# Sums of the up-projection's weights made ahead of time on GpSimd and kept in DRAM, and gate weights in three smaller buffers

## The chip, the cores and the metric

One core of one Trainium2 chip runs the whole program. Its engines work side by side: TensorE (PE, with PEld for its weight loads), VectorE (DVE), ScalarE (ACT), GpSimd (POOL) and SyncE (SP), which here issues every DMA. Each engine takes its instructions strictly in order, and an instruction that waits for a semaphore holds everything behind it on its engine; SP's list of DMAs is such a queue too. The metric is the device time of one execution in microseconds. Lower is better.

## The reference

One layer of a bidirectional encoder on two sequences of 512 tokens, width 1024, in float32:

```python
h = rmsnorm(x, g_attn) * (1 + sc1) + sh1
z = h @ w_in                                  # mixers A and B, and two gates of 1024 columns each
oa = window_attention(rope(qa), rope(ka), va) # mixer A: 8 heads, 2 key heads, band of +-128
ob = dense_attention(qb, kb, vb)              # mixer B: 8 heads, low-rank q and kv, full 512 x 512
mix = sigmoid(gla) * (oa @ w_o_a) + sigmoid(glb) * (ob @ w_o_b)
x = x + gt1 * (mix @ w_out)
h2 = rmsnorm(x, g_ffn) * (1 + sc2) + sh2
u = dwconv(h2 @ w_up, conv_w, conv_b)         # w_up: 1024 x 5632, convolution of width 3 over tokens
ua, ug = split(u)                             # 2816 columns each
x = x + gt2 * ((silu(ug) * ua) @ w_down)
```

## The kernel before

**Products.** Every large product is made of three TensorE products of float32r operands: each operand is split into a rounded high part and the rest, and high x high, high x low and low x high are added up in PSUM. A split is a cast or copy for the high part (ACT, or POOL at line 69) and a subtraction for the rest (DVE, or POOL at line 72 or 922).

**Stages, in order.** Input projection of mixers A and B (0 to about 216 us of the span); attention of both mixers, with the gates' projection woven in (to about 584 us); branch outputs, gated sum and output projection (to about 767 us); up-projection with convolution and gating (to about 1211 us); down-projection.

**Attention.** The work goes by units: one unit is one head and 128 queries, 64 units of mixer B (`PairB`) and then 64 of mixer A (`GroupA`). A unit's scores go to PSUM; DVE takes the maximum (L501), ACT the exponential (L504), DVE the reciprocal of the sum (L505), and POOL multiplies the row by it (L506, tile `p`). TensorE transposes `p` (L512) `LAG = 3` units after the scores. Between them `fill(5)` puts five matmuls of the gate projection (`psg`, L491) into every unit. The gate weights come in halves of 128 columns, `wg_raw`, 512 KB each; POOL splits each by two L69 and two L72 instructions. Before, two buffers hold a pair of halves each.

**Up-projection.** The two sequences and the two halves of the weights are multiplied with seven products in place of eight, for each of 22 blocks `c` of 128 columns. Four of the seven weight operands are sums of the four quarters a1, a2 (of the value half) and g1, g2 (of the gate half): `sf[0] = g1 + g2`, `sf[1] = sf[0] - a1`, `sf[2] = a1 - g1`, `sf[3] = a2 - sf[1]`. `weights_rest` (L931 to L943) makes them on POOL, 128 x 512 each, then `split_w` (L919) casts on ACT (L921) and subtracts on DVE or POOL (L922). The results `px`, `py`, `pz` are copied out of PSUM by ACT (`copied`, L960), convolved (L966 to L969), gated and stored to `g_d`. Raw weights pass through six buffers `wraw`, split ones through eight, `wt`. The first two products of blocks 0 to 3 are made early (`EARLY`), so right after that four blocks of five products each follow one another.

**What sets the order.** The text above is written in one order, but a scheduler lays out each engine's list in advance: by its own estimates of durations it takes, whenever an engine is idle, the next instruction whose inputs are there. So an instruction that is ready early moves far ahead of its place in the text. The lists are fixed on the chip. A buffer that is used in turn makes its next writer wait for its last reader: the load of a tile waits for the store of the tile two before it, where there are two buffers.

Of the kernel before, what the change touches and what calls it, by code (L numbers as in the profile page):

```python
# [8 lines left out]
F32 = mybir.dt.float32  # L9
F32R = mybir.dt.float32r  # L10
# [7 lines left out]
NB = 2  # L18
S = 512
TOK = NB * S  # L20
NT = S // 128
KD = D // 128
# [11 lines left out]
NP = FF // 128  # L34
# [5 lines left out]
def encoder_block(ctx, tc, x, c_t, w_ada0, b_col, w_ada, b_ada, cols, w_z, w_g, gains, tabs, sink,  # L40
# [11 lines left out]
    g_d = dram.tile([NB, NP, 128, S], F32, name="g_d")  # L52
    x1_d = dram.tile([TOK, D], F32, name="x1_d")
    gt_d = dram.tile([2, NB, D], F32, name="gt_d")

    ident = const.tile([128, 128], F32, name="ident")
    make_identity(nc, ident)
# [10 lines left out]
    def split_pool(hi, lo, raw, in_order=False):  # L68
        ins = G.tensor_scalar(out=hi, in0=raw, scalar1=1.0, scalar2=0.0, op0=ALU.mult, op1=ALU.add)  # L69
        if in_order:  # L70
            tc.keep_in_program_order(ins)
        G.tensor_sub(lo, raw, hi.bitcast(F32))  # L72
# [389 lines left out]
    with ExitStack() as st:  # L462
# [6 lines left out]

        def gates():  # L470

            def load(f):
                w = gw.tile([128, 2, 2, KD, 128], F32R, name=f"wg{f % 2}")
                for m in range(2):
                    raw = gw.tile([128, KD, 128], F32, name="wg_raw", bufs=2)
                    SY.dma_start(raw, w_g[f, :, m])
                    for k in range(0, KD, 4):
                        split_pool(w[:, 0, m, k:k + 4], w[:, 1, m, k:k + 4], raw[:, k:k + 4])
                return w

            w_next = load(0)
            for f in range(KD):
                w = w_next
                for q in range(4):
                    m, b = divmod(q, 2)
                    if q == 1 and f + 1 < KD:
                        w_next = load(f + 1)
                    ps = psg.tile([128, S], F32, name="psg")
                    for k in range(KD):
                        for n, (wl, hl) in enumerate(((0, h_hi), (0, h_lo), (1, h_hi))):  # L490
                            PE.matmul(ps, lhsT=w[:, wl, m, k, :], rhs=hl[b][:, k, :],  # L491
                                      start=k == 0 and n == 0, stop=k == KD - 1 and n == 2)
                            yield
                    go = gw.tile([128, S], F32, name="go", bufs=2)
                    A.copy(go, ps)
                    SY.dma_start(gate_d[b, f, :, m], go)

        def softmax(ps, n, plen):

# [179 lines left out]

        blocks = [PairB(b, g) for b in range(NB) for g in range(BH // 2)] + [GroupA(b, g) for b in range(NB) for g in range(AKV)]  # L680
        gate = gates()

        def fill(n):
            for _ in range(n):
# [8 lines left out]
        for n in range(len(todo) + LAG + 2):  # L693
            if n < len(todo):
                blk, u, first = todo[n]
                if first:
                    for _ in nxt:
                        pass
                    bi, since = blocks.index(blk), 0
                    nxt = blocks[bi + 1].prep() if bi + 1 < len(blocks) else iter(())  # L700
                scored.append((blk, u, blk.scores(u)))
            fill(5)
            for blk_, h in heads:
                blk_.values(h)
            heads = []
            if scored and (n >= LAG):
                blk_, u_, p_ = scored.pop(0)
                h = blk_.spread(u_, p_)
                if h is not None:
                    heads.append((blk_, h))  # L710
            if n < len(todo):
                if since >= blk.prep_from:
                    next(nxt, None)
                since += 1
        for _ in gate:
            pass


# [4 lines left out]
        return pm.tile([128, 512], F32, name=name, tag="bank")  # L723

    def wraw(src):
        r = wp.tile([128, 512], F32, name="wraw", bufs=6)
        SY.dma_start(r, src)
        return r

# [86 lines left out]
    with ExitStack() as s0:  # L816
        wk = s0.enter_context(tc.tile_pool(name="wkx", bufs=1))

        def tmp(tag):
            return wk.tile([128, S], F32, name=f"tmp_{tag}", bufs={"cc": 6, "sf": 5}.get(tag, 2))  # L820

        x1 = [mblk("x1_0", "st", [128, NT, D], F32), mblk("x1_1", "pt", [128, NT, D], F32)]
        ss = wk.tile([128, 2 * NT, 2], F32, name="ss2")
# [98 lines left out]
            lo_eng.tensor_sub(w[:, 1], raw, w[:, 0].bitcast(F32))  # L922
            return w.rearrange("p a (k n) -> p a k n", k=4)

        def weights_first(c):
            for q in range(2):
                yield split_w(wraw(w_up[c, 0, q]), G)

        def weights_rest(c, raws=None):  # L931
            a1, a2 = raws or (wraw(w_up[c, 0, 0]), wraw(w_up[c, 0, 1]))
            g1, g2 = wraw(w_up[c, 1, 0]), wraw(w_up[c, 1, 1])
            sf = [tmp("sf") for _ in range(4)]
            G.tensor_add(sf[0], g1, g2)
            G.tensor_sub(sf[1], sf[0], a1)
            yield split_w(sf[1], V)
            yield split_w(sf[0], V)
            G.tensor_sub(sf[2], a1, g1)
            yield split_w(sf[2], V)  # L940
            G.tensor_sub(sf[3], a2, sf[1])
            yield split_w(sf[3], V)
            yield split_w(g2, G)  # L943

        def weights_all(c):
            raws = (wraw(w_up[c, 0, 0]), wraw(w_up[c, 0, 1]))
            for r in raws:
                yield split_w(r, G)
            yield from weights_rest(c, raws)

        def product(ps, w, name, add=False, sl=slice(0, S)):
            for i in range(4):
# [191 lines left out]
```

## Time and profile before

| what | value |
|---|---|
| time, median of 3 runs (lowest to highest) | 1456.73 us (1453.19 to 1458.41) |
| time of the profiled execution | 1456.77 us |
| its span, first to last instruction | 1455.0 us |
| busy, share of the span | PE 96%, PEld 79%, DVE 69%, ACT 47%, POOL 41% |
| mean granted TensorE clock | 0.992 of full speed |
| read from and written to device memory | 148.39 MB and 44.06 MB |

TensorE is busy nearly everywhere, so the interest lies in the few stretches where it is not, and in what the other engines still have free beside it. A row that gives a line (L922) gives a line of the kernel before; a releaser, as in "<-POOL tmp_sf L936", is what ended an idle time. Matmul durations in the rows overlap: 128 x 512 matmuls follow one another faster than the duration of one says.

### The profile page before, as it was taken

The numbers are of one execution on the slowest core, as the hardware profiler recorded it, in microseconds if no ns is written. First come the engines' busy times: TensorE is split into PE (matmuls) and PEld (weight loads), VectorE is DVE, ScalarE is ACT, GpSimd is POOL, SyncE is SP. The second block draws the span as 40 slices with busy tenths as digits, with TensorE's granted clock in tenths as the row PEclk, the third lists the DMA queues.
The fourth block names the chain that finished last, engine by engine and source line by source line (L and its number), as shares of the span: only waits on it lengthen the run. The fifth ranks groups of instructions, "written<-read, shape, count | busy, mean of one in ns | idle before, by whom it ended". The sixth has DMA issues, their size and how long they took to land.

```text
span 1455.0 us, 20795 instructions
## 1 busy us (share of the span) xinstructions
PE 1391.8 (96%) x7184; PEld 1153.1 (79%) x7184; DVE 1000.3 (69%) x1907; ACT 679.3 (47%) x1385; POOL 596.0 (41%) x592
## 2 busy tenths in 40 slices
PE   5888998999999999999998899999999999999998
PEld 4777776888888888878887767888888888888887
DVE  5788776666678886545479888777777787447433
ACT  3475223666666665422347455555555554212210
POOL 3174023442433442381005755555555545544430
PEclk9999999999999999999999999999999999999999
DMA  8565763322222213655312322222222327646522
GB/s 342 176 216 170 236 239 135 116 88 87 88 87 73 102 64 120 236 176 200 133 39 73 120 74 87 87 82 85 87 85 82 102 73 250 205 148 223 180 87 73
DMA packets 107801, 193.82 MB, mean 133 GB/s; under 512 B 18856, under 2 KB 39592, under 8 KB 104624
## 3 DMA queue, kind: packets, MB, share of 16 engines
q1 hardware_dynamic: 107696, 192.49, 39.8%
q8 instruction: 57, 0.93, 0.3%
q14 instruction: 48, 0.39, 0.1%
HBM read 148.39 MB, written 44.06 MB: 132 GB/s over the span
## 4 chain that ended last, share of the span: by engine, by line
PE 77%; DVE 13%; POOL 3%; ACT 2%; DMA 2%; issue 2%; SPq 0%; ACTq 0%; POOLq 0%; DVEq 0%
PE px L955 13%; PE psg L491 11%; PE py L955 7%; PE psd L79 5%; PE psd L80 5%; PE psd L81 5%; PE pz L955 3%; PE ppt L512 3%; PE ppo L575 2%; PE psx L81 2%; PE psx L80 2%; PE psx L79 2%; PE psz L79 2%; PE psy L81 1%; PE psy L79 1%
## 5 line engine op out<-in xcount | busy, mean ns | idle before, releaser
L955 PE MATMUL px<-t,wt 128*128 128x512 f32 x792 | 191.2, 391 | 7.0 <-ACT tmp_cc L960 6.3
L922 POOL TENSOR_TENSOR wt<-wraw,wt 128x512 fp32r<-128x512 f32 x66 | 92.8, 1410 | 232.2 <-ACT wt L921 232.0
L955 PEld LDWEIGHTS px<-t,wt 128*128 128x128 f32 x792 | 148.0, 188 | 41.1 <-ACT tmp_cc L960 9.5
L491 PE MATMUL psg<-h_hi,wg 128*128 128x512 f32 x512 | 170.2, 397 | 0.0
L506 POOL TENSOR_SCALAR p<-p,l 128x512 f32<-128x512 f32 (+2 forms) x128 | 78.8, 617 | 200.3 <-DVE l L505 125.7
L76 DVE TENSOR_TENSOR wd<-wraw,wd 128x512 fp32r<-128x512 f32 x88 | 93.1, 1098 | 96.4 <-ACT wd L75 96.4
L79 PE MATMUL psd<-wd 128*128 128x512 f32 x352 | 136.9, 389 | 0.0
L80 PE MATMUL psd<-wd 128*128 128x512 f32 x352 | 136.9, 389 | 0.0
L81 PE MATMUL psd<-wd 128*128 128x512 f32 x352 | 136.9, 389 | 0.0
L75 ACT CAST wd<-wraw 128x512 fp32r<-128x512 f32 x88 | 51.3, 620 | 156.1 <-issue 86.9
L491 PEld LDWEIGHTS psg<-h_hi,wg 128*128 128x128 f32 x512 | 95.9, 189 | 18.4 <-POOL wg L69 0.8
L491 PE MATMUL psg<-h_lo,wg 128*128 128x512 f32 x256 | 101.8, 397 | 0.0
L504 ACT ACTIVATE p<-pps,nm 128x512 f32<-128x512 f32 (+2 forms) x128 | 78.2, 611 | 39.3 <-DVE nm L501 31.7
L922 DVE TENSOR_TENSOR wt<-tmp_sf,wt 128x512 fp32r<-128x512 f32 x88 | 82.2, 944 | 12.2 <-ACT wt L921 12.0
L967 DVE SCALAR_TENSOR_TENSOR tmp_u<-tmp_cc,cw,tmp_u 128x511 f32<-128x511 f32 x66 | 64.3, 974 | 37.3 <-ACT tmp_u L966 37.2
L69 POOL TENSOR_SCALAR wd<-wraw 128x512 fp32r<-128x512 f32 x44 | 34.2, 777 | 112.0 <-PE psd L81 63.9
L81 PEld LDWEIGHTS psd<-wd 128*128 128x128 f32 x352 | 66.1, 188 | 13.8
L79 PEld LDWEIGHTS psd<-wd 128*128 128x128 f32 x352 | 66.1, 188 | 13.7
L80 PEld LDWEIGHTS psd<-wd 128*128 128x128 f32 x352 | 66.1, 188 | 13.6
L501 DVE TENSOR_REDUCE nm<-pps 128x1 f32<-128x512 f32 (+2 forms) x128 | 74.7, 584 | 3.1 <-PE pps L81 1.5
L966 ACT ACTIVATE tmp_u<-tmp_cc,cw 128x512 f32<-128x512 f32 x66 | 53.6, 813 | 45.7 <-DMA g_d<-tmp_u 25.6
L72 POOL TENSOR_TENSOR wd<-wraw,wd 128x512 fp32r<-128x512 f32 x44 | 72.7, 1653 | 3.7
(257 smaller groups left out, 3517.8 us busy)
## 6 DMA issues: line engine op xcount, KB each, us to landing
w_ada<-in_w_ada_dram SPq DMA_DIRECT2D x24, 1024.0 KB, 7.1
wraw<-in_w_up_dram SPq DMA_DIRECT2D x96, 256.0 KB, 2.7
wraw<-in_w_down_dram SPq DMA_DIRECT2D x88, 256.0 KB, 3.6
g_d<-tmp_u SPq DMA_DIRECT2D x44, 256.0 KB, 2.4
wraw<-g_d SPq DMA_DIRECT2D x44, 256.0 KB, 2.7
wg_raw<-in_w_g_dram SPq DMA_DIRECT2D x16, 512.0 KB, 3.7
gate_d<-go SPq DMA_DIRECT2D x32, 256.0 KB, 2.0
ldb<-qb_d SPq DMA_DIRECT2D x8, 1024.0 KB, 4.9
```

The costliest lines, as they stand in the source:

```text
L72: G.tensor_sub(lo, raw, hi.bitcast(F32))
L76: V.tensor_sub(lo, raw, hi.bitcast(F32))
L79: PE.matmul(ps, lhsT=lh, rhs=rh, start=first, stop=False)
L80: PE.matmul(ps, lhsT=lh, rhs=rl, start=False, stop=False)
L81: PE.matmul(ps, lhsT=ll, rhs=rh, start=False, stop=last)
L491: PE.matmul(ps, lhsT=w[:, wl, m, k, :], rhs=hl[b][:, k, :], start=k == 0 and n == 0, stop=k == KD - 1 and n == 2)
L501: V.tensor_reduce(nm, ps[:, :n], op=ALU.max, axis=AX.X, negate=True)
L504: A.activation(p[:, :n], ps[:, :n], AF.Exp, bias=nm, accum_out=l)
L506: G.tensor_scalar(out=p[:, :plen], in0=p[:, :plen], scalar1=l, scalar2=1.0, op0=ALU.mult, op1=ALU.mult)
L922: lo_eng.tensor_sub(w[:, 1], raw, w[:, 0].bitcast(F32))
L955: PE.matmul(ps[:, sl], lhsT=w[:, wl, i], rhs=h[:, hl, sl], start=not add and i == 0 and n == 0, stop=i == 3 and n == 2, skip_group_check=add)
L967: V.scalar_tensor_tensor(out=u[:, 1:S], in0=src[:, 0:S - 1], scalar=cw[:, cc, 0:1], in1=u[:, 1:S], op0=ALU.mult, op1=ALU.add)
```

## The change

A new generator `weight_sums` loads the four quarters of each block `c` in two pieces of 128 x 4 x 256 (512 KB, a tile `wsum` with two buffers), makes the four sums in place on POOL in four instructions of 128 x 256, each of which reads the one before, and stores the tile to a DRAM scratch `su_d` (512 KB). That is 44 pieces, 176 POOL instructions, 44 loads and 44 stores. It is advanced 45 times in the attention's loop. The up-projection then loads five tiles for each block in place of two or four (three of w_up and four of `su_d` in all), the sum `sf[3]` has its rest made by POOL and not by DVE, and POOL's 88 sums of 128 x 512 are gone from that stage. `wraw` has seven buffers, and the tag `sf` four, not five. The gate weights go by halves, in three buffers of one half each in place of two of two.

```diff
@@ attention @@
+    su_d = dram.tile([NP, 128, 4, 512], F32, name="su_d")
...
-            def load(f):
-                w = gw.tile([128, 2, 2, KD, 128], F32R, name=f"wg{f % 2}")
-                for m in range(2):
+            ws = []
+
+            def load():
+                n = len(ws)
+                if n < 2 * KD:
+                    w = gw.tile([128, 2, KD, 128], F32R, name="wg", bufs=3)
                     raw = gw.tile([128, KD, 128], F32, name="wg_raw", bufs=2)
-                    SY.dma_start(raw, w_g[f, :, m])
+                    SY.dma_start(raw, w_g[n // 2, :, n % 2])
                     for k in range(0, KD, 4):
-                        split_pool(w[:, 0, m, k:k + 4], w[:, 1, m, k:k + 4], raw[:, k:k + 4])
-                return w
+                        split_pool(w[:, 0, k:k + 4], w[:, 1, k:k + 4], raw[:, k:k + 4])
+                    ws.append(w)
...
+        def weight_sums():
+
+            def sums(c, cs, t):
+                G.tensor_add(t[:, 3], t[:, 2], t[:, 3])
+                G.tensor_sub(t[:, 2], t[:, 0], t[:, 2])
+                G.tensor_sub(t[:, 0], t[:, 3], t[:, 0])
+                G.tensor_sub(t[:, 1], t[:, 1], t[:, 0])
+                SY.dma_start(su_d[c, :, :, cs], t)
+
+            last = None
+            for c in range(NP):
+                for q in range(2):
+                    cs = slice(256 * q, 256 * (q + 1))
+                    t = gw.tile([128, 4, 256], F32, name="wsum", bufs=2)
+                    SY.dma_start(t, w_up[c].rearrange("m q p n -> p (m q) n")[:, :, cs])
+                    if last:
+                        sums(*last)
+                    last = (c, cs, t)
+                    yield
+            sums(*last)
+            yield
...
+            if n >= 2 and (n - 2) * (2 * NP + 1) // 124 != (n - 3) * (2 * NP + 1) // 124:
+                next(wsum, None)
@@ up-projection @@
-        r = wp.tile([128, 512], F32, name="wraw", bufs=6)
+        r = wp.tile([128, 512], F32, name="wraw", bufs=7)
...
-        def weights_rest(c, raws=None):
-            a1, a2 = raws or (wraw(w_up[c, 0, 0]), wraw(w_up[c, 0, 1]))
-            g1, g2 = wraw(w_up[c, 1, 0]), wraw(w_up[c, 1, 1])
-            sf = [tmp("sf") for _ in range(4)]
-            G.tensor_add(sf[0], g1, g2)
-            G.tensor_sub(sf[1], sf[0], a1)
-            yield split_w(sf[1], V)
-            yield split_w(sf[0], V)
-            G.tensor_sub(sf[2], a1, g1)
-            yield split_w(sf[2], V)
-            G.tensor_sub(sf[3], a2, sf[1])
-            yield split_w(sf[3], V)
-            yield split_w(g2, G)
+        def weights_rest(c):
+
+            for q, eng in ((0, V), (3, V), (2, V), (1, G)):
+                yield split_w(wraw(su_d[c, :, q]), eng)
+            yield split_w(wraw(w_up[c, 1, 1]), G)
```

The lists of instructions show where the scheduler put the new work. POOL in mixer B's attention, before: 19 rows of `p` follow one another between two halves of gate weights.

```order
L506 TENSOR_SCALAR p<-p,l 128x512
L69 TENSOR_SCALAR wg_3321<-wg_raw 128x512 x2
L72 TENSOR_TENSOR wg_3321<-wg_raw,wg_3321 128x512 x2
L506 TENSOR_SCALAR p<-p,l 128x512 x19
L69 TENSOR_SCALAR wg_3976<-wg_raw 128x512 x2
```

The same engine in the same stage now (L534 is the old L506, L70 and L73 are the old L69 and L72), from the fourteenth unit on: two pieces of sums stand between three `p` and the next.

```order
L534 TENSOR_SCALAR p<-p,l 128x512 x3
L507 TENSOR_TENSOR wsum<-wsum 128x256
L508 TENSOR_TENSOR wsum<-wsum 128x256
L509 TENSOR_TENSOR wsum<-wsum 128x256
L510 TENSOR_TENSOR wsum<-wsum 128x256
L507 TENSOR_TENSOR wsum<-wsum 128x256
L508 TENSOR_TENSOR wsum<-wsum 128x256
L509 TENSOR_TENSOR wsum<-wsum 128x256
L510 TENSOR_TENSOR wsum<-wsum 128x256
L70 TENSOR_SCALAR wg<-wg_raw 128x512 x2
L534 TENSOR_SCALAR p<-p,l 128x512
L73 TENSOR_TENSOR wg<-wg_raw,wg 128x512
```

Counted over POOL's whole list, 12 sums stand ahead of the first `p`, 11 more ahead of the eighth, 136 (after those 12) ahead of the sixty-fourth, which is the last of mixer B, and 164, all of them, ahead of the eightieth. The sums have moved ahead of their places in the loop, where 23 pieces would have been passed at the end of mixer B.

SP's list in mixer B's attention, now (L566 is the load of a pair's q, k and v, L500 the store of a gate tile, L480 the load of a gate half, L609 the store of an attention output):

```order
L566 DMA ldb<-qb_d 128x4x512
L500 DMA gate_d<-go 128x512
L518 DMA wsum<-in_w_up_dram 128x4x256
L511 DMA su_d<-wsum 512x1x256
L480 DMA wg_raw<-in_w_g_dram 128x1024
L511 DMA su_d<-wsum 512x1x256
L518 DMA wsum<-in_w_up_dram 128x4x256
L609 DMA o_d<-o 128x512
L518 DMA wsum<-in_w_up_dram 128x4x256
L511 DMA su_d<-wsum 512x1x256
L500 DMA gate_d<-go 128x512
```

Between two stores of gate tiles there stood one to three DMAs before; now there are six to eight, and the loads of `ldb`, the gate weights and the pieces wait for one another in one list.

ACT at the start of the up-projection, before, with what each row waits for:

```order
L921 CAST wt<-tmp_sf 128x512 [waits Pool_49]
L921 CAST wt<-tmp_sf 128x512
L921 CAST wt<-tmp_sf 128x512 [waits PE_49,Pool_49]
L960 COPY tmp_cc<-px 128x512 [waits PE_49]
L921 CAST wt<-tmp_sf 128x512 [waits Pool_49]
```

The same place now (L954 is the old L921, L981 the old L960):

```order
L954 CAST wt<-wraw 128x512 [waits DMAHW0_49,Pool_49]
L954 CAST wt<-wraw 128x512 [waits DMAHW1_49,Pool_49]
L954 CAST wt<-wraw 128x512 [waits DMAHW2_49,Pool_49]
L954 CAST wt<-wraw 128x512 [waits DMAHW3_49,PE_49,Pool_49]
L981 COPY tmp_cc<-px 128x512 [waits PE_49]
```

The casts ahead of the copy wait for a DMA that brings a finished sum, and no longer for POOL's sum. POOL is still named where the buffer `wt` must come free.

## Rows read from the trace of the kernel before

**Rows 1.** The page's first line: the span of the profiled execution.
```profile
span 1455.0 us, 20795 instructions
```

**Rows 2.** Windows: length, then busy us by engine, PEclk, DMA share, GB/s.
```profile
240.00:422.00 182.00, 182.00 (x977) 152.12 (x977) 122.44 (x240) 118.56 (x254) 65.67 (x86) 1.00 0.27 92
801.00:900.00 99.00, 90.22 (x386) 71.49 (x385) 84.87 (x93) 50.97 (x87) 63.47 (x39) 1.00 0.30 95
900.00:1211.00 311.00, 310.34 (x1368) 256.43 (x1367) 241.46 (x282) 170.86 (x280) 159.66 (x115) 1.00 0.29 90
```

**Rows 3.** Timeline of TensorE in the up-projection: start us, us, what, [idle before <-releaser].
```profile
810.18 3.02 PE L955 MATMUL px<-t,wt 128*128 128x512 f32 x12 [2.65 <-ACT tmp_cc L960]
821.20 2.88 PE L955 MATMUL py<-t,wt 128*128 128x512 f32 x12
823.92 2.88 PE L955 MATMUL px<-t,wt 128*128 128x512 f32 x12
```

**Rows 4.** Timeline of ScalarE at the same place.
```profile
805.66 1.14 ACT L921 CAST wt<-tmp_sf 128x512 fp32r<-128x512 f32 x2 [4.08 <-POOL tmp_sf L936]
809.55 0.58 ACT L960 COPY tmp_cc<-px 128x512 f32<-128x512 f32 x1
```

**Rows 5.** Groups of instructions, 801 to 900 us: busy, mean ns, idle before.
```profile
L936 POOL TENSOR_TENSOR tmp_sf<-tmp_sf,wraw 128x512 f32<-128x512 f32 x7 | 12.9, 1847 | 5.9 <-issue 5.6
L921 ACT CAST wt<-tmp_sf 128x512 fp32r<-128x512 f32 x24 | 14.5, 616 | 8.9 <-POOL tmp_sf L936 6.1 <-POOL tmp_sf L939 2.2 <-POOL tmp_sf L941 0.6
L966 ACT ACTIVATE tmp_u<-tmp_cc,cw 128x512 f32<-128x512 f32 x15 | 12.2, 812 | 21.2 <-DVE tmp_cc L1006 11.5 <-DMA g_d<-tmp_u 9.7
L967 DVE SCALAR_TENSOR_TENSOR tmp_u<-tmp_cc,cw,tmp_u 128x511 f32<-128x511 f32 x16 | 18.2, 1134 | 10.0 <-ACT tmp_u L966 10.0
L967 DVE SCALAR_TENSOR_TENSOR tmp_u<-px,cw,tmp_u 128x511 f32<-128x511 f32 x5 | 3.7, 741 | 0.0
```

**Rows 6.** Groups of GpSimd's instructions, 240 to 422 us.
```profile
L506 POOL TENSOR_SCALAR p<-p,l 128x512 f32<-128x512 f32 x62 | 43.2, 698 | 119.0 <-DVE l L505 98.8 <-PE pps L81 19.0 <-PE ppt L620 1.0
L72 POOL TENSOR_TENSOR wg<-wg_raw,wg 128x512 fp32r<-128x512 f32 x12 | 15.3, 1290 | 0.1
L69 POOL TENSOR_SCALAR wg<-wg_raw 128x512 fp32r<-128x512 f32 x12 | 7.8, 661 | 3.7 <-PE psg L491 3.7
```

**Rows 7.** By line, scores of both mixers: ns min/median/max, first and last start.
```profile
L79 PE MATMUL pps<-qk x64: 393/481/503, 240.0 to 421.9; 96*128 96x512 f32 x64
L646 PE MATMUL pps<-sta x128: 274/339/440, 426.5 to 561.9; 128*128 128x256 f32 x64, 128*128 128x384 f32 x64
```

**Rows 8.** By tile, two-input operations of GpSimd, 512 and 256 columns.
```profile
L72 POOL TENSOR_TENSOR wg<-wg_raw,wg x32: 1263/1287/1588, 211.6 to 520.4; 128x512 fp32r<-128x512 f32 x32
L327 POOL TENSOR_TENSOR qf<-t1b,t2b x8: 737/741/926, 83.2 to 140.1; 128x256 f32<-128x256 f32 x8
```

**Rows 9.** DMA issues: count, KB each, median us from issue to landing.
```profile
wg_raw<-in_w_g_dram SPq DMA_DIRECT2D x16, 512.0 KB, 3.7
gate_d<-go SPq DMA_DIRECT2D x32, 256.0 KB, 2.0
qb_d<-qf SPq DMA_DIRECT2D x8, 384.0 KB, 3.3
qb_d<-vf SPq DMA_DIRECT2D x8, 256.0 KB, 5.4
```

**Rows 10.** Timeline of TensorE and GpSimd around one unit of mixer B.
```profile
307.79 0.48 PE L79 MATMUL pps<-qk 96*128 96x512 f32 x1
312.50 0.69 POOL L506 TENSOR_SCALAR p<-p,l 128x512 f32<-128x512 f32 x1 [5.61 <-DVE l L505]
318.49 0.60 PE L512 MATMUL ppt<-ident,p 128*128 128x128 f32 x4
```

**Rows 11.** Groups of GpSimd's instructions, 422 to 584 us.
```profile
L506 POOL TENSOR_SCALAR p<-p,l 128x384 f32<-128x384 f32 x32 | 18.8, 589 | 33.8 <-DVE pps L650 14.2 <-DVE l L505 13.4 <-PE pps L646 3.8
L506 POOL TENSOR_SCALAR p<-p,l 128x256 f32<-128x256 f32 x32 | 15.4, 482 | 42.7 <-DVE pps L650 28.4 <-DVE l L505 8.8 <-PE pps L646 3.1
```


## Prediction of the time after the change

> **What bounds the kernel now.** I read the span first: 1455.0 us of the execution's 1456.77, so 1.8 lie around it [rows 1]; that execution stands 0.04 us above the median of the runs, and sums against it need no shift. Then I cut the span into windows [rows 2]. The reader is to see TensorE's sum against each window's length. In mixer B's attention (240 to 422) PE is busy 182.00 of 182.00: a microsecond by which anything holds PE there is lost, because PE has no idle time later in the stage to catch up. From 801 to 900, the start of the up-projection, it is busy 90.22 of 99.00. The idle part understates the loss, since a matmul's row covers some of its own waiting: in undisturbed stretches twelve matmuls take 823.92 - 821.20 = 2.72 us [rows 3], 0.2267 each, so 386 of them are 87.5 us of work and 11.5 us are lost. From 900 to 1211 it is 310.34 of 311.00: nothing is to be had there. The change thus takes work out of a stage that loses 11.5 us and puts work under one that loses nothing.
>
> **What it removes: POOL's sums in the up-projection.** The timeline shows how PE loses time there: it idles 2.65 us before 810.18 for ACT's copy L960 [rows 3]. ACT had itself stood 4.08 us for POOL's sum L936 in front of the cast at 805.66, and the copy, behind that cast on the same engine, ran at 809.55 [rows 4]. In the groups of this window ACT waits 6.1 + 2.2 + 0.6 = 8.9 us for POOL sums [rows 5]. After the change these casts wait for a load, and the tiles are there long before, so this chain goes. What is late next is the convolution: ACT's L966 waits 21.2 us, 11.5 on DVE and 9.7 on the store of g_d, and DVE's L967 takes 1134 ns when both inputs lie in SBUF, 741 when one is in PSUM, while POOL's sum takes 1847 [rows 5] against 1287 for such an operation of 512 columns elsewhere [rows 8]. So the sums also slowed DVE, and both get faster; the waits on g_d stay. Of the 11.5 us only the first stall's 2.65 is traced directly to a sum: the bounds are a gain of 3 and of 11.5. I take 9, since ACT's 8.9 us on POOL are the nearest row. The five products per block need five loads for four; the seventh wraw buffer and the fourth sf tile change nothing that waits. Moving the rest of sf[3] to POOL costs POOL less than the four sums it loses.
>
> The Trainium skill ("SBUF — State Buffer", section "Who interferes with whom") states that a VectorE operation with two SBUF inputs and a GpSimd operation that reads SBUF exclude each other for a whole instruction. The trace agrees with 1134 against 741 ns. By the rule all of DVE's excess would go with the sums, and the gain would be nearer 11.5 than 9. It also speaks against the change in the attention, but there DVE's large operations read a PSUM operand, and the rule exempts those.
>
> **What it adds: 176 sums of 128x256 on POOL in the attention.** PE's work there is unchanged; what can hold it is `p`, which POOL delivers. POOL works in 240 to 422 for 65.67 us [rows 2] and stands 98.8 us waiting for DVE's `l` [rows 6]; that idle time is the cover. A unit of mixer B takes (421.9 - 240.0)/63 = 2.887 us, one of mixer A (561.9 - 426.5)/63 = 2.15 [rows 7].
>
> The price of a sum: a two-input operation of 256 columns takes 737 to 926 ns, median 741 [rows 8]. Four in a chain, reading what the one before wrote, are not shown; I take 0.80, near the median, and keep 0.74 and 0.93. A piece of four is then 3.2 us.
>
> The instruction lists (section on the change) put 136 - 11 = 125 sums between the eighth and sixty-fourth `p`. That is 125 x 0.80 = 100.0 us, with 56 `p` at 0.698 = 39.1 [rows 6] and 21 gate-weight operations at 1.29 and 0.66 [rows 6] = 20.8: 160 us of POOL work in 56 x 2.887 = 161.7 us. So the arithmetic alone fills POOL to 99%, and any wait in its list lands on `p`.
>
> Such a wait is there. The two buffers of `wsum` make the load of a piece wait for the store of the piece two before it. A store and a load, one behind the other: 512 KB of gate weights land in 3.7 us; stores took 2.0 (256 KB), 3.3 (384 KB in 768-byte pieces, nearest to ours of 1 KB) and 5.4 us (256 KB) [rows 9]. So a buffer is away 3.3 + 3.7 = 7.0 us, with bounds 5.7 and 9.1. Meanwhile POOL has what stands in its list between the two pieces: the other piece and the `p` and gate operations. Summed over the list for the 31 pieces that begin there, this is 4.6 us at least (3.2 and two `p`), 6.7 in the mean, 10.6 at most; 21 fall short of 7.0, by 33.6 us together (10.5 at 5.7, 79.5 at 9.1). A wait for one buffer lies partly inside the other's absence, so between half and all of that counts, 17 to 34; I take two thirds, 23. The list then lasts 160 + 23 = 183 us against 161.7, 21 late. The slack of `p` comes off: scores at 307.79, `p` done at 313.19, transposed at 318.49 [rows 10], 5.3 us. Mixer B ends **16 us later**.
>
> Behind the POOL instruction that waits for a piece stand the next `p` and gate operations, and PE waits for both. SP is in the same lock-step: a store that waits for POOL holds the `ldb`, gate-weight and gate-tile DMAs behind it, so a late POOL also delays the inputs of the next pair.
>
> Mixer A's units 65 to 80: 28 sums are 22.4 us, 16 `p` at 0.589 and 0.482 are 8.6 [rows 11], eight gate operations 7.8: 38.8 us in 16 x 2.15 = 34.4, so 4.4 over, and two buffer waits at about 0.8 = 1.6: **6 us more**. After the eightieth `p` no sum is left, and PE, full before, gives nothing back. Together 22; the bounds are 0 (10.5 x 2/3 = 7 late, less 1.7 of room and 5.3 of slack) and 60 (79.5 x 2/3 = 53 late makes 46 in mixer B, about 14 in mixer A).
>
> The Trainium skill ("DMA: Bandwidth & Descriptors", section "Anatomy of one DMA") gives a transfer about 2.0 us and its bytes at 436 GB/s, stated for DMAs that GpSimd issues, not SyncE. That makes 512 KB an estimated 3.2 us each way, 6.4 per absence, and mixer B's delay some 5 us less. The gate weights' 3.7 are measured and decide.
>
> **Edits at nothing.** Gate weights by halves: the same splits by the same lines, and three halves ahead in place of four; the 98.8 us hide it, and if POOL is full they are late with `p`, inside the sum above. 44 loads and 44 stores of 512 KB are 46 MB more through DMA engines that are busy 0.27 of the stage [rows 2]; if they did collide, wg_raw's 3.7 would stretch, which the bound of 9.1 holds.
>
> **Sum.** 1456.8 + 16 + 6 - 9 = 1469.8, so **1470 us**.
>
> **The rivals.** *The sums fit* (faster). If a sum takes 0.74 and the absence is 5.7, POOL has 125 x 0.74 + 59.9 = 152.4 us of work and 7 of waiting in 161.7; the lateness stays under the slack, mixer A's 37 us in 34 likewise, and the gain stays: 1457 - 6 to 1457 - 11, 1446 to 1451. For it: 98.8 us of idle POOL, and waits that the scheduler could spread. Against it: 99% by the median-like price.
> *The buffers lock step* (much slower). A piece goes load, wait, four sums, store, wait, on two buffers, with SP's single list between them: if a store's issue waits behind a load that waits for the other store, absences grow past 9.1. It decides from an absence of about 8.5 us on; at 9.1 and above the attention loses 35 to 67, less 9: 1482 to 1515. For it: 5.4 us for 256 KB of stores, and six to eight DMAs between two gate stores; against it: most stores took 2.0 to 3.3.
> *The terms cancel.* An attention that loses 5 to 13 us against the same 9: 1453 to 1461, within the 0.3% (4.4 us) that a measurement of this kernel can tell from no change. It needs an absence of about 6.2.
> *The change misses its aim*: should the stall at 810 have been DVE's, only 3 would be gained, and the forecast is 1476; that lies inside its own range and takes no chance of its own.
>
> **How the numbers follow.** Forecast (attention +15 to +40, gain 3 to 11): 0.47, own range 1460 to 1485. Lock step 0.15, sums fit 0.24, cancelling 0.14. Faster by over 0.3% is 0.24, within 0.14, slower 0.47 + 0.15 = 0.62. The range must leave out 2 in 10: below 1447 lies a quarter of the fitting case, 0.06, and above 1500 somewhat under half of the lock step, 0.06; 1447 to 1500 leaves out less, 0.12, since both unknown bounds, absence and price, are open.
>
> **What would show it.** Right: POOL over 95% busy or waiting on the DMA of `wsum` in mixer B, PE idle before the transposes with POOL's `p` as releaser, mixer B longer than 182 us by about 16 and mixer A by 6; sums near 0.80 us, loads of pieces near 3.7, stores near 3.3; the first blocks of the up-projection losing 2 or 3 us rather than 11.5, and ACT's casts waiting for no sum. Wrong: PE at 100% in the attention with the up-projection's gain kept (the sums fit); stores near 2 us; or sums of 0.74 us and less. If the first blocks stay 11 us long with no sum in sight, the loss there was the convolution's.

## The result and the profile after

The changed kernel takes 1518.57 us (median of 4 runs, 1517.53 to 1519.81) against 1455.66 us before: 1.0435 times as long, 95% interval 1.0414 to 1.0457. That is 63 us more; the forecast was 1470, its range 1447 to 1500. The profiled execution has a span of 1518.0 us.

The first look goes to windows of the changed kernel: mixer B (first scores to mixer A's first scores), mixer A (to the branch outputs), the 99 us of the up-projection that answer to 801 to 900 of before [rows 2], and the whole up-projection. The columns are those of [rows 2].

```profile
236.70:479.50 242.80, 207.45 (x1001) 167.03 (x1002) 127.10 (x246) 121.87 (x259) 165.52 (x225) 0.92 0.68 220
479.50:654.40 174.90, 160.57 (x868) 135.45 (x866) 125.06 (x373) 100.99 (x262) 84.90 (x126) 0.96 0.40 132
874.80:973.80 99.00, 99.00 (x437) 81.68 (x436) 70.22 (x95) 57.80 (x95) 28.75 (x22) 1.00 0.45 139
841.70:1274.00 432.30, 425.95 (x1912) 354.06 (x1913) 296.71 (x405) 245.74 (x414) 132.59 (x100) 0.99 0.42 129
```

The same cuts in the kernel before, mixer B, mixer A and the up-projection:

```profile
240.00:426.50 186.50, 186.50 (x1000) 155.88 (x1001) 125.73 (x246) 121.29 (x259) 67.06 (x88) 1.00 0.26 89
426.50:584.00 157.50, 155.74 (x867) 131.78 (x866) 125.33 (x373) 100.82 (x262) 62.04 (x94) 1.00 0.29 98
768.00:1211.00 443.00, 428.75 (x1912) 353.32 (x1913) 358.16 (x428) 244.13 (x413) 244.26 (x165) 0.99 0.29 91
```

So mixer B is 56.3 us longer, mixer A 17.4, the up-projection 10.7 shorter, the stages between 3.3 longer and the one ahead 3.3 shorter: 63.0. In mixer B PE is idle for 242.80 - 207.45 = 35.4 us, and its 1001 matmuls are busy for 21 us longer than the 1000 of before, since the granted clock there is 0.92 on average and was 1.00. The up-projection's first 99 us now hold 437 matmuls, where 386 ran before; 437 x 0.2267 = 99.1.

What holds PE in the attention, and what SyncE (SPq) waits for in mixer B, from the views of waits (us in total, times, longest), PE first:

```profile
PE ppt L540 <- POOL p L534: 38.3, 17, 5.3
PE ppo L603 <- ACT p L542: 8.1, 2, 4.8
PE ppt L579 <- DMA ldb<-qb_d: 1.5, 1, 1.5
```

```profile
SPq L511 <- POOL wsum L510: 83.5, 28, 4.6
SPq L518 <- DMA su_d<-wsum: 35.9, 17, 5.9
SPq L511 <- DMA wsum<-in_w_up_dram: 34.6, 16, 6.9
SPq L480 <- POOL wg L73: 15.5, 6, 5.4
```

PE's idle time is for the most part GpSimd's `p`, as forecast. GpSimd's groups from the start of the eighth `p` to the end of the sixty-fourth (262.95 to 482.23 us) show why `p` is late:

```profile
L534 POOL TENSOR_SCALAR p<-p,l 128x512 f32<-128x512 f32 x57 | 40.1, 714 | 2.4 <-DVE l L533 2.4
L510 POOL TENSOR_TENSOR wsum<-wsum 128x256 f32<-128x256 f32 x32 | 23.7, 740 | 2.3
L507 POOL TENSOR_TENSOR wsum<-wsum 128x256 f32<-128x256 f32 x31 | 22.7, 732 | 60.0 <-DMA wsum<-in_w_up_dram 59.9
L508 POOL TENSOR_TENSOR wsum<-wsum 128x256 f32<-128x256 f32 x31 | 22.7, 732 | 2.2
L509 POOL TENSOR_TENSOR wsum<-wsum 128x256 f32<-128x256 f32 x31 | 22.7, 731 | 2.2
L73 POOL TENSOR_TENSOR wg<-wg_raw,wg 128x512 fp32r<-128x512 f32 x12 | 15.7, 1321 | 0.0
L70 POOL TENSOR_SCALAR wg<-wg_raw 128x512 fp32r<-128x512 f32 x10 | 6.1, 622 | 0.0
```

The busy column adds up to 153.7 us; the view's own sum, without overlaps, is 150.3, and about 80 ns stand between dependent sums, 6.7 us in the last column. That is the forecast's 160 us of work, within 3. The rest is 59.9 us of waiting for pieces, where the forecast had 23. GpSimd waits for `l` for 2.4 us, where it waited 98.8 [rows 6]: GpSimd's list is now what sets mixer B's length, and PE's slower clock lies beneath it.

One such wait, in the timelines of GpSimd and SyncE (start, duration, and in brackets the idle time before; rows in between are left out of the first):

```profile
257.45 0.74 POOL L510 TENSOR_TENSOR wsum<-wsum 128x256 f32<-128x256 f32 x1
260.50 1.21 POOL L70 TENSOR_SCALAR wg<-wg_raw 128x512 fp32r<-128x512 f32 x2
263.61 1.29 POOL L73 TENSOR_TENSOR wg<-wg_raw,wg 128x512 fp32r<-128x512 f32 x1
265.57 2.04 POOL L534 TENSOR_SCALAR p<-p,l 128x512 f32<-128x512 f32 x3
274.04 0.74 POOL L507 TENSOR_TENSOR wsum<-wsum 128x256 f32<-128x256 f32 x1 [6.42 <-DMA wsum<-in_w_up_dram]
```

```profile
258.22 0.52 SPq L511 DMA_DIRECT2D su_d<-wsum  x1
258.79 0.62 SPq L500 DMA_DIRECT2D gate_d<-go  x1
264.93 0.34 SPq L480 DMA_DIRECT2D wg_raw<-in_w_g_dram  x1
265.36 0.39 SPq L566 DMA_DIRECT2D ldb<-qb_d  x1
265.84 0.46 SPq L518 DMA_DIRECT2D wsum<-in_w_up_dram  x1
```

The buffer's sums end at 258.19 and its store is issued at once. Its next load is not issued when the store lands, some 3.4 us later, but at 265.84: ahead of it on SyncE stands the load of gate weights, which goes out only at 264.93, when GpSimd has ended the split at 263.61 that frees its buffer. The piece is there at 274.04. So the buffer was away for 15.8 us, while GpSimd, on whose split SyncE had waited, waited 6.42 us for it with `p` behind. Read in this way, the fifteen waits above 0.3 us in this stretch follow absences of 6.7 to 17.8 us, median 10.1; the forecast had 7.0, its bounds 5.7 and 9.1. Here it is a load of gate weights that stands ahead. In eleven of the fifteen it is the store of the other piece, which waits for that piece's last sum on GpSimd (the 83.5 us of the row SPq L511 above are such waits), in four of these for little; in three nothing but the landing of its own store holds the load.

The DMA issues (KB each, median us to landing) explain a part of it: the loads of pieces take 5.0 us, though 512 KB of gate weights took 3.7 [rows 9].

```profile
wsum<-in_w_up_dram SPq DMA_DIRECT2D x44, 512.0 KB, 5.0
su_d<-wsum SPq DMA_DIRECT2D x44, 512.0 KB, 3.4
wg_raw<-in_w_g_dram SPq DMA_DIRECT2D x16, 512.0 KB, 4.6
ldb<-qb_d SPq DMA_DIRECT2D x8, 1024.0 KB, 6.8
```

### The profile page after: what moved, and what is told of

It reads as the page before. It is cut to its first block, busy times and chain, and to the rows that moved or that the text cites. A ratio compares the mean times of both kernels' runs of the same rounds, so it can differ in the third digit from the quotient of the medians.

```text
span 1518.0 us, 21184 instructions
## 1 busy us (share of the span) xinstructions
PE 1417.5 (93%) x7184; PEld 1169.0 (77%) x7184; DVE 943.2 (62%) x1885; ACT 680.7 (45%) x1385; POOL 609.8 (40%) x702
## 4 chain that ended last, share of the span: by engine, by line
PE 67%; DVE 9%; POOL 9%; DMA 9%; issue 2%; ACT 2%; SPq 1%; POOLq 0%; ACTq 0%; DVEq 0%
PE px L976 15%; PE py L976 8%; PE psg L495 6%; DMA wsum<-in_w_up_dram 6%; PE psd L80 5%; PE psd L82 5%; PE psd L81 5%; PE pz L976 4%; PE psx L81 2%; PE psx L80 2%; PE psx L82 2%; PE ppt L540 1%; POOL wsum L508 1%; POOL wsum L507 1%; POOL wsum L509 1%
## 5 line engine op out<-in xcount | busy, mean ns | idle before, releaser
L955 POOL TENSOR_TENSOR wt<-wraw,wt 128x512 fp32r<-128x512 f32 x88 | 118.9, 1356 | 400.4 <-ACT wt L954 382.5
L495 PE MATMUL psg<-h_hi,wg 128*128 128x512 f32 x512 | 176.4, 411 | 0.0
L495 PEld LDWEIGHTS psg<-h_hi,wg 128*128 128x128 f32 x512 | 100.3, 198 | 19.9 <-POOL wg L73 0.8
L954 ACT CAST wt<-wraw 128x512 fp32r<-128x512 f32 x154 | 93.9, 618 | 39.4 <-POOL wt L955 26.5
L540 PE MATMUL ppt<-ident,p 128*128 128x128 f32 x416 | 71.9, 289 | 38.5 <-POOL p L534 38.3
L495 PE MATMUL psg<-h_lo,wg 128*128 128x512 f32 x256 | 105.4, 412 | 0.0
L534 POOL TENSOR_SCALAR p<-p,l 128x512 f32<-128x512 f32 (+2 forms) x128 | 79.0, 624 | 64.4 <-DVE pps L678 30.4
L540 PEld LDWEIGHTS ppt<-ident,p 128*128 128x128 f32 x416 | 54.9, 148 | 61.5 <-POOL p L534 47.7
L988 DVE SCALAR_TENSOR_TENSOR tmp_u<-tmp_cc,cw,tmp_u 128x511 f32<-128x511 f32 x66 | 57.3, 869 | 42.0 <-ACT tmp_u L987 42.0
L70 POOL TENSOR_SCALAR wd<-wraw 128x512 fp32r<-128x512 f32 x44 | 33.7, 766 | 112.5 <-PE psd L82 84.6
```

Of the source, the lines that this page charges most:

```text
L495: PE.matmul(ps, lhsT=ws[n][:, wl, k, :], rhs=hl[b][:, k, :], start=k == 0 and i == 0, stop=k == KD - 1 and i == 2)
L534: G.tensor_scalar(out=p[:, :plen], in0=p[:, :plen], scalar1=l, scalar2=1.0, op0=ALU.mult, op1=ALU.mult)
L540: PE.transpose(pt[:, j * 128:(j + 1) * 128], p[:, j * 128:(j + 1) * 128], ident)
L954: A.copy(w[:, 0], raw)
```

## The experiments

Three theories. L: the round trip of a piece (store, load, and what stands between them on SyncE) makes GpSimd wait. S: GpSimd's own work is packed too densely for PE's pace. T: 46 MB of traffic delay what PE needs. Where an expectation gives the attention as 322 us, it counts from the first scores to the last. A label such as e4 is the run's name. Lengths by stage, from the first matmuls of each stage in the profiles, in us; the ratio is to the kernel before on the same chip:

| kernel | mixer B | mixer A | up-projection | span | ratio (95%) |
|---|---|---|---|---|---|
| before | 186.5 | 157.5 | 443.0 | 1455.0 | 1 |
| changed | 242.8 | 174.9 | 432.3 | 1518.0 | 1.0435 (1.0414 to 1.0457) |
| e1 no sums | 204.4 | 159.6 | 432.3 | 1463.7 | 1.0055 (1.0035 to 1.0075) |
| e2 up-projection only | 189.5 | 157.3 | 431.4 | 1445.9 | 0.9935 (0.9913 to 0.9957) |
| e3 no store | 239.8 | 157.3 | 431.7 | 1496.0 | 1.0294 (1.0270 to 1.0317) |
| e4 held at their places | 190.3 | 180.9 | 432.4 | 1475.6 | 1.0115 (1.0095 to 1.0134) |
| e5 the same, 3 buffers | 189.3 | 171.9 | 432.3 | 1462.3 | 1.0030 (1.0017 to 1.0043) |
| e6 free to move, 3 buffers | 230.3 | 164.8 | 433.0 | 1495.9 | 1.0262 (1.0235 to 1.0290) |
| e7 first four blocks | 189.3 | 157.3 | 435.3 | 1451.6 | 0.9973 (0.9956 to 0.9989) |
| e8 gate halves alone | 189.6 | 157.3 | 443.5 | 1460.4 | 1.0012 (0.9998 to 1.0025) |
| e9 four blocks, old gates | 187.6 | 158.5 | 435.8 | 1447.2 | 0.9949 (0.9932 to 0.9966) |
| e10 eight blocks, old gates | 188.5 | 162.7 | 432.2 | 1453.5 | 0.9965 (0.9954 to 0.9976) |
| e11 one sum at a time, 3 buffers | 189.0 | 164.3 | 432.4 | 1454.9 | 1.0001 (0.9985 to 1.0017) |
| e12 the changed kernel's pace, 3 buffers | 206.6 | 161.7 | 433.0 | 1467.4 | 1.0086 (1.0053 to 1.0118) |
| e13 the same, 2 buffers | 236.8 | 173.1 | 432.6 | 1513.2 | 1.0379 (1.0340 to 1.0417) |

**e1, no sums.** The four `G.tensor_...` lines of `sums` are deleted.

> The 176 sums on GpSimd are left out; all 44 loads and 44 stores of the pieces stay, so the scratch holds the raw quarters and the up-projection runs on them with the same instructions. Theory L (round trip): what costs 74 us in the attention is GpSimd waiting for a piece whose buffer is away for its store and load, with p queued behind it. Without sums nothing on GpSimd waits for a piece: attention back to about 322 us, up-projection's gain kept, time 1443 to 1449. Theory S (GpSimd's own arithmetic fills it): the same 1443 to 1449, since the arithmetic is gone too. Theory T (traffic: 46 MB more slow the loads that TensorE needs, or SyncE's list holds them): the attention stays longer by 20 us or more, time above 1465, with TensorE waiting on DMAs.

1465.27 us, which is not what L and S had; it lies at the lower edge of T's numbers, with an attention 20 us longer than before. Without sums the scheduler sends the pieces back to back, 293 GB/s in mixer B, and that alone makes it 15 us longer than in e2 with the same instructions on PE (8.5 us of them idle time of PE, 6.4 its slower clock, 0.97 on average). The views of waits say what suffers, PE first, then ACT in mixer B:

```profile
PE ppo L599 <- ACT p L538: 7.5, 2, 4.8
PE ppt L575 <- DMA ldb<-qb_d: 5.5, 3, 2.2
```

```profile
ACT vsb L567 <- DMA ldb<-qb_d: 9.5, 3, 3.6
```

`ldb`, the load of a pair's q, k and v, lands 6.9 us after its issue (before 4.9). In the changed kernel it takes as long, 6.8, at 220 GB/s, but PE waits only 1.5 us for it there, while it waits for GpSimd. So T has a part that shows where GpSimd does not hold PE; in the changed kernel it is not what sets the time.

**e2, the up-projection's side alone.** No generator; and

```diff
-                yield split_w(wraw(su_d[c, :, q]), eng)
+                yield split_w(wraw(w_up[c, q // 2, q % 2]), eng)
```

> Only the up-projection's side of the change, with the gate weights by halves: no pieces, no sums, no scratch; the up-projection loads the raw quarters of the weights where the change loads sums (so the product is of other weights, in the same instructions). All theories: attention as before the change, 322 us, no loss; the up-projection's part 10 to 11 us shorter, as in the changed kernel, so 1443 to 1449. If the gain hung on the sums being early or on the gate halves, the time would lie within 3 us of 1456.

1448.29 us, as expected: the up-projection's gain is there by itself, 11.6 us, and the attention is nearly as before, 3 us longer in mixer B.

**e3, no store.** `SY.dma_start(su_d[c, :, :, cs], t)` is deleted, the up-projection as in e2.

> The 44 stores of the sums are left out (the up-projection loads raw quarters in their place); loads and all 176 sums stay, so a buffer is away for its load alone, about 5 us and not 9 to 18. The scheduler then moves the sums further ahead: about 130 stand between the eighth and the fortieth p, where 76 stood. Theory L: the waits for pieces fall from 77 us to under 20, and the attention loses less than 15 us: 1446 to 1460. Theory S: there GpSimd has 130 sums at a pitch of 0.81, 32 p at 0.69 and 18 gate operations, about 145 us of work in 32 x 2.887 = 92 us of TensorE's, so mixer B ends 40 us late or more with hardly a wait for a DMA: 1480 to 1495. Theory T: about 23 MB are gone, half of the 74 us at most comes back: about 1480, with waits on DMAs.

1500.09 us: S, and a little above its numbers. GpSimd waits for pieces for only 6.0 us in the attention, and yet mixer B takes 239.8, because 130 sums now stand between the eighth and the fortieth `p`. GpSimd is the bound there from 266 to 405 us (window as above):

```profile
266.00:405.00 139.00, 108.18 (x507) 85.79 (x508) 63.75 (x122) 61.34 (x129) 128.91 (x177) 0.91 0.58 187
```

The run does not tell what the round trip costs in the changed kernel, for a shorter trip let the scheduler pack the list more densely: one bound took the place of the other.

**e4, the sums held at their places.** Each of the four calls is kept where the text has it:

```diff
-                G.tensor_add(t[:, 3], t[:, 2], t[:, 3])
+                tc.keep_in_program_order(G.tensor_add(t[:, 3], t[:, 2], t[:, 3]))
```

> The changed kernel whole, with one difference: the sums are held at their places in the text, so that they are spread evenly over the 128 units (84 ahead of the sixty-fourth p, where 148 stood). A piece then comes every 2.76 units, 8.0 us in mixer B and 5.9 in mixer A, and with two buffers one may be away for 12.8 and 8.7 us. Theory L as a matter of pace: the absence of 8.4 to 9 us fits in mixer B and just about in mixer A; 0 to 10 us lost in the attention, 1446 to 1456. Theory L as a lock step of SyncE's list, whatever the pace: waits for pieces above 40 us and a time above 1490. Theory S: 1446 to 1452, because GpSimd has 146 us of work in mixer B's 185. Theory T: traffic is the same as now, so 1500 or more.

1473.73 us. Mixer B came out as L had it for its pace (190.3 us), mixer A did not: 23 us lost, with 38.4 us of waiting for pieces in the attention as a whole. "Just about" was too hopeful for an absence of 8.4 us and more against the 8.7 that are free there. S (1446 to 1452) missed it too, and so did T: all 44 loads and 44 stores are still made, and the time is 45 us below the changed kernel's.

**e5, the same with a third buffer**, paid for with one buffer less of `o`.

> The sums held at their places in the text as in the pinned run, with three buffers for the pieces in place of two (paid for by one buffer, not two, of the attention's output tile o). In the pinned run mixer B was nearly whole and mixer A lost 23 us, with 38 us of GpSimd waiting for pieces. In mixer A a piece comes every 2.76 x 2.15 = 5.9 us, so with two buffers one may be away for 8.7 us, with three for 14.6; the measured absence is 8.4 us and more. Theory L: the waits for pieces fall below 10 us and mixer A's loss below 8, time 1448 to 1460. Theory S: GpSimd has 92 sums at 0.81, 64 p and the gate operations there, some 129 us of work in 138, so most of the loss stays whatever the buffers: 1465 or more.

1464.29 us. The waits fell to 4.8 us, as L said, and 9 us of mixer A came back; 14 stayed, which L did not say, and the time lies between L's range and S's. Both theories have a share in mixer A.

**e6, the changed kernel with a third buffer**, sums free to move.

> The changed kernel with three buffers for the pieces (and one for the tile o), the sums free to move. The list now has 152 sums between the eighth and the sixty-fourth p, where 125 stood. Theory L: the waits for pieces fall from 77 us to under 25 and the attention's loss from 74 to under 25: below 1475. Theory S: the list itself is 152 x 0.81 + 39 + 21 = 183 us long against 161.7, so at least 16 us stay even with no wait, and each wait comes on top; with waits of 10 to 30 us the attention loses 25 to 45: 1473 to 1493.

1497.07 us, beyond both. The waits fell only to 32.6 us, and the list grew by 27 sums: like e3 it gives back one thing and takes another.

**e7, the first four blocks alone.** `range(NP)` becomes `range(4)` in the generator, with the sums held and one piece in seven units; `weights_rest` loads sums for `c < 4` and makes them itself for the others.

> Sums ahead of time for the first four blocks c alone (8 pieces, 32 sums, held at their places, one piece in seven units of mixer B); the other 18 blocks make their sums in the up-projection, as before the change. If the up-projection's gain of 11 us lies in the first blocks, as the forecast had it, it is all kept (up-projection 432 to 434 us, before 443), and the attention loses 0 to 3 us: 1444 to 1450. If the gain were spread over all blocks, four of 22 would bring 2 us: 1453 to 1457.

1454.21 us, 0.9973 of before. As a whole that is where the expectation put a gain spread over all blocks, but the stages say otherwise: the up-projection keeps 7.7 us of its gain with 32 of 176 sums, where an even share would be 2, so most of it does lie in the first blocks, though not all as expected. The attention lost about 3 us all the same.

**e8, the gate halves alone** in the kernel before.

> The kernel before with the gate weights by halves in three buffers, and nothing else. My forecast had this edit at nothing: 1454 to 1459, mixer B at 186 to 187 us. The run of the up-projection's side alone had mixer B 3 us longer (189.5 against 186.5) with the halves in it: if they are the cause, 1457 to 1461 and mixer B near 189.

1461.53 us, 1.0012, not told apart from no change as a whole; mixer B's 189.6 us in the profile is the same 3 us that e2 and e7 have. The edit that the forecast had at nothing costs about that; by what path was not traced.

**e9 and e10, old gate weights; four and eight blocks.** The gates' code of before, `wsum` and `o` with one buffer each.

> The sums of the first four blocks alone ahead of time, at their places (one piece in seven units), as in the run of the first four, but with the gate weights as they were before the change (two buffers of a pair of halves); one buffer for the pieces and one for the tile o pay for it. A piece comes every 20 us in mixer B, so one buffer that is away for 9 to 18 us holds nothing. If the gate halves were what made mixer B 3 us longer, mixer B is 186 to 187.5 us and the whole attention 344 to 345, the up-projection 435 as in the first-four run: 0.992 to 0.996 of the kernel before. If the 3 us came from the pieces or the one list of DMAs, mixer B stays at 189 to 190: 0.995 to 0.998.

> The same with eight blocks, one piece in seven units through both mixers (16 pieces, 64 sums). The first-four run kept 8 of the 11 us of the up-projection (435.3 against 432.3, before 443.0). If the other 3 lie in blocks 4 to 7, the up-projection comes to 432 to 433 and the time to 0.990 to 0.994 of before; if they lie in none in particular, it stays at 435, as with four. Theory S: in mixer A a piece comes every 15 us and costs GpSimd 3.2, nowhere near full: the attention loses 0 to 2 us.

e9 is the fastest of the kernels that leave nothing out (e2, which makes no sums, is faster): 1450.24 us against 1458.40 of before on the same chip, 0.9949, some 7 us faster. Its mixer B at 187.6, a tenth above the expected range, confirms the gate halves in the main; the whole attention, 346.1, is 1 us above its range. e10 reaches 432.2 us in the up-projection, so the other 3 us do lie in blocks 4 to 7, but it loses 4 to 5 in mixer A, where a piece in 15 us seemed free, and misses its range: 0.9965. Of this loss PE's waits for `p` there, 2.2 us, show a part; the rest stays open.

**e11, one sum at a time.** As e5, with a `yield` after each sum and 1.42 sums to a unit.

> All 176 sums at their places with three buffers, as in the pinned run with three, but handed out one at a time (1.42 per unit) and not four in a row. That run still lost 15 us in mixer A with 5 us of waits for pieces. If what is left there is lumps (four sums of 3.2 us and gate operations of 4 us in front of one p), mixer A falls from 172 to 158 to 164 us and the time to 1450 to 1457. If it is theory S, GpSimd's work as a whole (129 us in 138), it stays above 167: 1459 to 1466.

1457.28 us, 1.0001: all 176 sums, and all 88 DMAs, at no net cost. Mixer A falls from 171.9 to 164.3, just above the expected range: half of what e5 still lost was four sums in a row ahead of one `p`.

**e12 and e13, the changed kernel's own density.** The sums are held, but the generator is advanced so that they stand as densely as the scheduler had put them (22 ahead of the eighth `p`, 148 of the sixty-fourth; changed kernel 23 and 148). e12 has three buffers, e13 two.

```diff
+            while made < len(ahead) * 16 and 4 * (made - 1) < ahead_of(n + 1):
+                next(wsum, None)
+                made += 1
```

> The sums held at the pace at which the changed kernel has them (12 ahead of the first p, 22 of the eighth, 148 of the sixty-fourth, 176 of the eightieth; in the changed kernel 12, 23, 148, 176), with three buffers for the pieces (and one for the tile o). So GpSimd's list is that of the changed kernel in mixer B, 126 sums at 0.81, 57 p and 22 gate operations, about 160 us from the eighth to the sixty-fourth p, and only the round trip differs. Theory L: of the changed kernel's 60 us of waits in that stretch under 15 are left, mixer B takes 190 to 203 us (changed kernel 243, before 186.5), time 1455 to 1475. Theory S: what matters is how densely the list is packed, and 160 in 162 is too dense whatever the buffers: mixer B above 215, time above 1485.

> The same held pace with two buffers for the pieces and two for the tile o, as the changed kernel has them: the control for the run with three. Both theories: as the changed kernel, 1505 to 1525, mixer B 232 to 248, with 45 to 70 us of waits for pieces in it. If holding the sums at their places helps by itself, it lies below 1495, and the run with three buffers is to be read against it and not against the changed kernel.

This settles it. With two buffers the time is 1512.69 us, nearly the changed kernel's, and GpSimd waits 76.2 us for pieces in the attention. With three it is 1468.72 and the waits are 14.5, at the same density of the list. What GpSimd loses to the round trip with two buffers costs 44 us. (e12 has one buffer less of `o` as well, which was not tried alone.) The first row is e13's, the second e12's:

```profile
POOL wsum L507 <- DMA wsum<-in_w_up_dram: 76.2, 23, 7.1
```

```profile
POOL wsum L507 <- DMA wsum<-in_w_up_dram: 14.5, 9, 3.1
```

Mixer B at 206.6 us is above the 203 that L allowed; PE waits there 5.5 us for `ldb` as in e1 (266 GB/s move in this stage): with GpSimd's waits gone, some of T shows again.

## Why the prediction was wrong

The direction, the mechanism and the place were right: GpSimd's list, `p` behind sums that wait for a piece, PE waiting for `p`, first in mixer B and then in mixer A's first units. One term was mis-sized: the absence of a buffer, and with it the waits for pieces.

*The gain.* Forecast 9 (3 to 11.5), measured 10.7, and 11.6 in e2. The stall's chain was right: ACT's casts no longer wait for a sum, and of PE's waits for ACT's copies, 6.3 + 2.4 us in the kernel before, 1.5 are left. PE's rows, two of before and two of after:

```profile
L955 PE MATMUL px<-t,wt 128*128 128x512 f32 x792 | 191.2, 391 | 7.0 <-ACT tmp_cc L960 6.3 <-DVE wt L922 0.6
L955 PE MATMUL py<-e,wt 128*128 128x512 f32 x264 | 63.8, 390 | 2.5 <-ACT tmp_cc L960 2.4
L976 PE MATMUL px<-t,wt 128*128 128x512 f32 x792 | 190.1, 389 | 1.5 <-ACT tmp_cc L981 1.5
L976 PE MATMUL py<-e,wt 128*128 128x512 f32 x264 | 63.4, 389 | 0.0
```

DVE's operation on two SBUF inputs fell from 1134 ns [rows 5] to 885 in the same 99 us:

```profile
L988 DVE SCALAR_TENSOR_TENSOR tmp_u<-tmp_cc,cw,tmp_u 128x511 f32<-128x511 f32 x18 | 15.9, 885 | 13.3 <-ACT tmp_u L987 13.3
```

The Trainium skill ("SBUF — State Buffer", section "Who interferes with whom") leads one to expect this; the trace agrees in direction, and not with the whole excess over 741. The prediction, which had all of the excess go with the sums, left out GpSimd's splits, which read SBUF as well: 22 of them (L955) run in these 99 us, 12 splits and 27 sums ran there before. That they are what is left of the excess was not tried. In the attention, where DVE's large operations read a PSUM operand, the sums did not slow them: L501's maximum took 681 ns before and after in mixer B, L515 690 before and 689 after.

*The work in mixer B.* Forecast 160 us from the eighth to the sixty-fourth `p`, measured 157 with the gaps. A sum takes 732 ns and 80 ns pass before the next: 0.81 for the forecast's 0.80.

*The step that failed:* "A wait for one buffer lies partly inside the other's absence, so between half and all of that counts, 17 to 34; I take two thirds, 23", on an absence of 7.0 us. The trace has 59.9 us of waits. The absence was taken as a store and a load back to back, and the load at the 3.7 us of the gate weights. It is a slower load (3.4 + 5.0 = 8.4 us by the landings) and, in twelve of the fifteen waits, the time that the load stands on SyncE behind a DMA which itself waits for GpSimd, from 0.5 to some 8 us: 10.1 us in the median, up to 17.8. The share of two thirds was not the error: worked out on the forecast's own list, an absence of 8.4 us for every piece makes 42 us of waits by that rule, one of 10.1 makes 71 (an estimate from the prices of the prediction). By the same list the absence of 6.4 us that the prediction mentions would have taken 8 us off the delay, not some 5. The forecast knew of the lock step of SyncE's list, but priced it only as a rival, from 8.5 us on, with a chance of 0.15 and 1482 to 1515. Such a lock step is what happened, with one difference: the rival had a store stand behind a load, and in these waits the load stands behind the other piece's store or the gate weights, which wait for GpSimd. Its price was still too low. And the bound of 9.1 us was no bound, since it was made of DMA durations alone, without a queue. The run e12 puts the number to it: with most of the waits gone (14.5 us are left) and the work as it was, the kernel takes 1468.7 us, against 1512.7 with two buffers (e13): 44 us are the round trip. That 1468.7 lies so near the forecast's 1470, which had 23 us of waits in it, is partly luck, for PE's 5.5 us of waiting for `ldb` and the 3 us of the gate halves are in e12 and stood at nothing in the forecast.

*Mixer A.* Forecast 6, measured 17.4, by the same step: GpSimd waited for five pieces there, 13 us of waits where 1.6 were counted.

*Edits at nothing.* The gate halves cost about 3 us in mixer B (e8; as a whole not told apart from no change). The traffic shows in the changed kernel as 1.5 us of PE's waits for `ldb`, and costs some 15 us in e1, where nothing else holds PE.

*Sums that would fit.* That rival fails as the code stands and holds when the sums are held at their places, one at a time, with three buffers (e11: 1.0001): GpSimd's free time was there, but the scheduler's list did not spread the work over it.

## What to carry to other kernels

Price a buffer's round trip as the store, the load, and everything that stands between the two on the issuing queue and may itself wait for the engine that is waiting: where two engines' lists wait for each other, durations of DMAs alone give no bound. Work put under a stage whose engine has slack wants to be held at an even pace, in small portions, or a scheduler may move it forward until that engine is full, as here (148 sums ahead of the sixty-fourth `p`, 84 when held). And before moving work of all blocks, see which blocks wait: here 32 of the 176 sums bring most of the gain, and with the gate weights left alone they make the kernel some 7 us faster than before.

## What the runs showed of the hardware

A load of 512 KB in pieces of 1 KB takes 5.0 us from issue to landing, where the same amount of gate weights took 3.7 with little else under way [rows 9] and 4.6 beside the pieces. The Trainium skill ("DMA: Bandwidth & Descriptors", section "Anatomy of one DMA") would give an estimated 3.2 us, for DMAs that GpSimd issues; the store's 3.4 is near it, the load is not, and the measurement decides. The 1 MB load of `ldb` went from 4.9 us with 89 GB/s moving in mixer B to 6.8 with 220 and 6.9 with 293. Where PE waited a few microseconds again and again, its granted clock fell too, from 2.4 to 1.2 GHz and back: after the 3.89 us for which it waited before 303.80 us a matmul of the scores took 0.78 us (granted clock 0.50 from 304 to 308 us), at 312.53 again 0.48 (1.00 from 312 to 316). Over mixer B the mean is 0.92, and the matmuls are busy for 21 us longer, which GpSimd's list, the longer one here, covers.
